# A decoder trunk with split float32 products: the low halves of the output weights by ACT and an adding transfer from POOL

## The chip, the core and the metric

The kernel runs on one core of a Trainium2 chip. The metric is the device time of one execution in microseconds (us). A core has five engines that run beside each other, each through its own queue in order: TensorE (PE, matmuls), VectorE (DVE), ScalarE (ACT), GpSimd (POOL) and SyncE (SP). Data moves between HBM, the large memory, and SBUF, the core's working memory, by transfers on 16 DMA engines; SP, ACT and POOL can issue them.

## What is computed

Two layers of a decoder over 256 positions of width 2048, float32. Layer 0 has sparse and sliding-window attention, layer 1 dilated attention; both end in an output projection, and each layer has an MLP:

```
def reference(x, positions, e_w_in, e_w_o, ..., o_w_in, o_w_o, ln1_g, ln1_b, mlp_w1, mlp_w2, ln2_g, ln2_b):
    ...
    for layer in range(DEPTH):
        ...
            y = _even_mixer(x, cos, sin, e_w_in[i], e_w_o[i], ...)   # ends in  o @ w_o
            y = _odd_mixer(x, cos, sin, o_w_in[i], o_w_o[i])         # ends in  o @ w_o
        x = _layer_norm(DN_ALPHA * x + y, ln1_g[layer], ln1_b[layer])
        x = _layer_norm(DN_ALPHA * x + _mlp(x, mlp_w1[layer], mlp_w2[layer]), ln2_g[layer], ln2_b[layer])
    return x
```

The change is about the two products `o @ w_o`, of a 256 x 2048 by a 2048 x 2048 matrix each.

## The kernel before, in words

Every large product is made of three matmuls in the number form F32R, which keeps fewer bits than float32. Each operand is split into a high half, its value rounded to F32R, and a low half, the rest: a x w is taken as a_hi w_hi + a_hi w_lo + a_lo w_hi. `hi_lo` (L122 to L124) does the split: ACT casts the source into the high half (L123), and DVE subtracts the high half from the source into the low half (L124).

The weights stream in chunks. `w_chunks` (L139) goes through the 2048 rows of a weight matrix, for a block of columns. For a block of 512 columns a chunk is 2 x 128 rows, for one of 256 columns 4 x 128 rows: always a tile of 128 partitions x 1024 numbers, 512 KB. For each chunk SP issues the load into a tile `raw` (L150), `hi_lo` writes `wh` and `wl`, and PE runs through it. `raw` has 5 buffers, `wh` and `wl` have 4 each; a step that writes a buffer waits until the last reader of its earlier content is done. `gemm_tok` (L160) runs the three matmuls for each 128 rows and each of the two halves of the 256 positions (L166 with wh, L167 with wl, L168 with wh): 12 matmuls of 512 columns a chunk, or 24 of 256 columns.

`project` (L665) is the output projection of a layer. It has three blocks of 512 columns of 8 chunks each, then `close` (L588). That first loads and splits the last 256 columns (`halves`, L560, by `hi_lo`), then runs one block of 256 columns (4 chunks), and then the last 256 columns from what `halves` prepared, with the layer norm between. Blocks thus make 28 chunks per layer through `w_chunks`. Between the chunks of the first block the generators in `later` (attention heads still to be finished) get their turn by `tick`, and `before` finishes a head when its rows are due. After each block DVE adds the result to the residual (`add_to`, L534).

The code is recorded once; a scheduler then sets each engine's order of instructions, which stays near the order of the code. A wait is a semaphore between engines.

Of the kernel before, what the change touches and what calls it, by code (L numbers as in the profile page):

```python
# [12 lines left out]
F32 = mybir.dt.float32  # L13
F32R = mybir.dt.float32r
I32 = mybir.dt.int32
AF = mybir.ActivationFunctionType
OP = mybir.AluOpType
# [70 lines left out]
def tile_hybrid_trunk(ctx: ExitStack, tc: tile.TileContext, x, positions, e_w_in, e_w_o, nsa_pe_k, nsa_pe_v,  # L88
# [3 lines left out]
    pe, act, dve, pool = nc.tensor, nc.scalar, nc.vector, nc.gpsimd  # L92
# [3 lines left out]
    wp = ctx.enter_context(tc.tile_pool(name="wp", bufs=W_BUFS))  # L96
# [10 lines left out]
    def tick(n):  # L107
        while n > 0 and later:
            try:
                next(later[0])  # L110
                n -= 1
            except StopIteration:
                later.popleft()

    def finish(gen):
        while gen in later:
            tick(1)
# [4 lines left out]
    def hi_lo(hi, lo, src):  # L122
        act.copy(hi, src)  # L123
        dve.tensor_tensor(lo, src, hi.bitcast(F32), op=OP.subtract)  # L124
# [4 lines left out]
    def hpair():  # L129
        return big.tile([128, 16, 2, T], F32R, name="hc")  # L130
# [5 lines left out]
        ts = slice(t * 128, t * 128 + 128)  # L136
        hi_lo(xc[:, c:c + n, 0, ts], xc[:, c:c + n, 1, ts], tp[:, :n])

    def w_chunks(w, row0, segs, order=range(16), before=None, ticks=None):  # L139
        n = sum(b for _, b in segs)  # L140
        ck = 4 if n <= 256 else 2
        order = list(order)
        for i in range(0, 16, ck):
            if before is not None:
                before(order[i:i + ck])
            r0 = row0 + order[i] * 128
            raw = wp.tile([128, ck, n], F32, name="raw", bufs=RAW_BUFS)
            o = 0
            for c0, b in segs:
                nc.sync.dma_start(raw[:, :, o:o + b], w[r0:r0 + ck * 128, c0:c0 + b]  # L150
                                  .rearrange("(a p) n -> p a n", p=128))
                o += b
            wh = wp.tile([128, ck, n], F32R, name="wh")
            wl = wp.tile([128, ck, n], F32R, name="wl")
            hi_lo(wh, wl, raw)
            for k in range(ck):
                yield order[i + k], i + k == 0, i + k == 15, wh[:, k], wl[:, k]
            tick(ticks or (1 if len(later) < LAG else 2))

    def gemm_tok(xc, w, row0, segs, **kw):  # L160
        n = sum(b for _, b in segs)
        acc = [ps.tile([128, 512], F32, name="acc")[:, :n] for _ in range(2)]
        for kt, first, last, wh, wl in w_chunks(w, row0, segs, **kw):
            for t in range(2):
                a, b = xc[:, kt, 0, t * 128:(t + 1) * 128], xc[:, kt, 1, t * 128:(t + 1) * 128]
                pe.matmul(acc[t], lhsT=a, rhs=wh, start=first, stop=False)  # L166
                pe.matmul(acc[t], lhsT=a, rhs=wl, start=False, stop=False)  # L167
                pe.matmul(acc[t], lhsT=b, rhs=wh, start=False, stop=last)  # L168
        return acc

    def gemm_feat(xc, w, row0, col0, n, **kw):
        acc = [ps.tile([128, 512], F32, name="acc") for _ in range(n // 128)]
        for kt, first, last, wh, wl in w_chunks(w, row0, [(col0, n)], **kw):
            for f in range(n // 128):
                fs = slice(f * 128, (f + 1) * 128)
                if not last:
                    pe.matmul(acc[f], lhsT=wh[:, fs], rhs=xc[:, kt], start=first, stop=False)  # L177
                pe.matmul(acc[f][:, 0:T], lhsT=wl[:, fs], rhs=xc[:, kt, 0], start=False, stop=False)  # L178
                if last:
                    pe.matmul(acc[f], lhsT=wh[:, fs], rhs=xc[:, kt], start=False, stop=True)  # L180
        return acc
# [124 lines left out]
    acc = gemm_tok(xc, e_in, 0, [(2048, 256), (3864, 256)], before=first)  # L306
# [9 lines left out]
    acc = gemm_tok(xc, e_in, 0, [(2304, 280)])  # L316
# [205 lines left out]
    oc = hpair()  # L522
# [11 lines left out]
    def add_to(acc, t, c0, n, fac, slot=None):  # L534
        z = xr[:, t, c0:c0 + n]
        dve.scalar_tensor_tensor(z, z, fac, acc, op0=OP.mult, op1=OP.add)  # L536
        if slot is not None:
            dve.bn_stats(st[t][:, slot], z)

    def load_gb(g_in, b_in, i):  # L540
        gb = big.tile([128, 2, D], F32, name="gb", tag="sgb")
        nc.sync.dma_start(gb[:, 0], g_in[i:i + 1].to_broadcast([128, D]))
        nc.sync.dma_start(gb[:, 1], b_in[i:i + 1].to_broadcast([128, D]))
        return gb
# [120 lines left out]
    def project(w, order, need, gin, bin_, i, nxt):  # L665
        def before(kts):
            if kts[0] in need:
                finish(need[kts[0]])

        def block(c0, n, slot):  # L670
            acc = gemm_tok(oc, w, 0, [(c0, n)], order=order, before=before, ticks=3)
            for t in range(2):
                add_to(acc[t], t, c0, n, ALPHA, slot)

        block(0, 512, 0)
        gb = load_gb(gin, bin_, i)
        block(512, 512, 1)
        block(1024, 512, 2)
        return close(oc, w, 0, ALPHA, gb, block, nxt)
# [53 lines left out]
    oc = hpair()  # L733
# [64 lines left out]
    for hb in range(4):  # L798
# [14 lines left out]
        for g in range(3):  # L813
            lo = 256 if hb + g == 0 else 0
            acc = gemm_tok(xc, o_in, 0, [(g * 6144 + 4096 + hb * 512 + lo, 512 - lo)])
# [34 lines left out]
```

## Time and profile before

| | |
|---|---|
| median of 2 runs | 2775.53 us (2775.29 to 2775.78) |
| span of the profiled execution | 2773.8 us |
| PE busy | 2748.2 us (99%) |
| DVE busy | 1686.6 us (61%) |
| ACT busy | 1239.0 us (45%) |
| POOL busy | 44.4 us (2%) |
| DMA moved | 509 MB, 184 GB/s in the mean |

The span is that of one execution with the profiler on; the median is of executions without it. An engine's busy time is the time in which it has an instruction under way; a matmul's own duration (0.39 us for 512 columns) overlaps its neighbours', so the pace is read from the starts, which are 0.227 us apart. "Idle before, releaser" says what ended an engine's wait. The DMA share is the mean busy share of the 16 DMA engines; it can come out a little above 1. The granted clock of PE is 1.00 at 2.4 GHz and 0.50 at 1.2 GHz.

### The profile page before, as it was taken

What the parts mean: (1) busy time and instruction counts of PE and PEld (TensorE: products, weight loads), DVE (VectorE), ACT (ScalarE), POOL (GpSimd) and SP (SyncE); (2) the same over time, 40 slices, a digit from 0 to 9 for tenths busy, and PEclk for the clock granted to TensorE, in tenths of its full rate; (3) what the DMA queues carried; (4) which work ended last, traced back from release to release, by engine and by line L of the source; (5) the groups of instructions that cost most, each with busy time, mean ns of one, the idle gap of its engine ahead of it and who ended that gap; (6) DMA issues with size and microseconds to landing.
All of it is one profiled execution on the core that took longest, in us unless ns stands there. A gap on an engine that the chain in (4) does not pass through costs nothing.

```text
span 2773.8 us, 37579 instructions
## 1 busy us (share of the span) xinstructions
PE 2748.2 (99%) x14840; PEld 2362.4 (85%) x14840; DVE 1686.6 (61%) x2281; ACT 1239.0 (45%) x1648; POOL 44.4 (2%) x40
## 2 busy tenths in 40 slices
PE   9999999999999999999999999999999999999997
PEld 7888888888888889888888888888898888888887
DVE  6667665455555556774774675576565455565556
ACT  5345444344443444444444445445444344443442
POOL 0000010000000001000000000000010000000001
PEclk9999999999999999999999999999999999999999
DMA  8743655665666665555555456455566665665653
GB/s 275 200 136 118 224 175 189 193 188 191 190 189 193 187 195 166 178 179 164 175 182 176 152 183 197 155 179 185 195 197 188 192 189 189 191 189 191 189 190 130
DMA packets 283985, 509.18 MB, mean 184 GB/s; under 512 B 15840, under 2 KB 61184, under 8 KB 282528
## 3 DMA queue, kind: packets, MB, share of 16 engines
q1 hardware_dynamic: 283248, 506.02, 58.9%
q8 instruction: 116, 1.90, 0.3%
q10 hardware_dynamic: 432, 0.59, 0.1%
q14 instruction: 61, 0.50, 0.0%
q0 software_dynamic: 128, 0.16, 0.0%
HBM read 504.62 MB, written 2.10 MB: 183 GB/s over the span
## 4 chain that ended last, share of the span: by engine, by line
PE 85%; issue 9%; DVE 1%; POOL 1%; ACT 0%; POOLq 0%
PE acc L177 28%; PE acc L178 15%; PE acc L168 12%; PE acc L166 12%; PE acc L167 12%; PE acc L180 2%; PE sc L743 1%; PE acc L586 1%; PE acc L584 1%; PE acc L585 1%; PE po L784 1%; PE tp L772 1%; DVE xr L621 0%; POOL xr L622 0%; PE po L780 0%
## 5 line engine op out<-in xcount | busy, mean ns | idle before, releaser
L124 DVE TENSOR_TENSOR wl<-raw,wh 128x1024 fp32r<-128x1024 f32 (+1 forms) x932 | 1133.2, 1220 | 941.0 <-ACT wh L123 938.5
L123 ACT CAST wh<-raw 128x1024 fp32r<-128x1024 f32 (+1 forms) x932 | 976.7, 1049 | 1327.1 <-PE acc L177 684.3
L177 PE MATMUL acc<-xc,wh 128*128 128x512 f32 x3690 | 1315.9, 400 | 1.1 <-DVE qk L185 1.1
L178 PE MATMUL acc<-xc,wl 128*128 128x256 f32 x3936 | 1094.1, 281 | 0.0
L177 PEld LDWEIGHTS acc<-xc,wh 128*128 128x128 f32 x3690 | 693.2, 188 | 166.6 <-DVE qk L185 1.8
L178 PEld LDWEIGHTS acc<-xc,wl 128*128 128x128 f32 x3936 | 743.4, 189 | 5.9
L166 PE MATMUL acc<-wh,hc 128*128 128x512 f32 (+1 forms) x1280 | 485.7, 379 | 0.0
L167 PE MATMUL acc<-wl,hc 128*128 128x512 f32 (+1 forms) x1280 | 484.7, 379 | 0.0
L168 PE MATMUL acc<-wh,hc 128*128 128x512 f32 (+1 forms) x1280 | 484.6, 379 | 0.0
L167 PEld LDWEIGHTS acc<-wl,hc 128*128 128x128 f32 x1280 | 240.8, 188 | 45.1
L168 PEld LDWEIGHTS acc<-wh,hc 128*128 128x128 f32 x1280 | 240.8, 188 | 44.9
L166 PEld LDWEIGHTS acc<-wh,hc 128*128 128x128 f32 x1280 | 240.9, 188 | 44.3
L166 PE MATMUL acc<-wh,xc 128*128 128x512 f32 (+2 forms) x448 | 170.4, 381 | 0.0
L167 PE MATMUL acc<-wl,xc 128*128 128x512 f32 (+2 forms) x448 | 168.6, 377 | 0.0
L168 PE MATMUL acc<-wh,xc 128*128 128x512 f32 (+2 forms) x448 | 168.0, 376 | 0.0
L166 PEld LDWEIGHTS acc<-wh,xc 128*128 128x128 f32 x448 | 84.6, 189 | 15.6 <-ACT xc L123 1.4
L168 PEld LDWEIGHTS acc<-wh,xc 128*128 128x128 f32 x448 | 84.6, 189 | 15.3 <-DVE xc L124 0.2
L167 PEld LDWEIGHTS acc<-wl,xc 128*128 128x128 f32 x448 | 84.7, 189 | 15.2 <-DVE wl L124 0.8
L180 PE MATMUL acc<-xc,wh 128*128 128x512 f32 x246 | 88.7, 395 | 0.0
L254 DVE TENSOR_TENSOR ropeB<-qk,sinT 64x512 f32<-64x512 f32 x120 | 82.3, 686 | 2.3
L536 DVE SCALAR_TENSOR_TENSOR xr<-xr,acc 128x512 f32<-128x512 f32 (+1 forms) x88 | 52.7, 633 | 23.6 <-PE acc L586 15.0
L184 ACT COPY qk<-acc 128x256 f32<-128x256 f32 x122 | 42.8, 373 | 30.8 <-PE acc L180 30.8
(187 smaller groups left out, 1491.4 us busy)
## 6 DMA issues: line engine op xcount, KB each, us to landing
raw<-in_mlp_w_dram SPq DMA_DIRECT2D x512, 512.0 KB, 3.8
raw<-in_o_w_in_dram SPq DMA_DIRECT2D x288, 512.0 KB, 3.7
raw<-in_e_w_in_dram SPq DMA_DIRECT2D x52, 512.0 KB, 4.4
raw<-in_e_w_o_dram SPq DMA_DIRECT2D x32, 512.0 KB, 3.6
raw<-in_o_w_o_dram SPq DMA_DIRECT2D x32, 512.0 KB, 4.5
raw<-in_e_w_in_dram SPq DMA_DIRECT2D x16, 256.0 KB, 6.2
gb<-in_ln_g_dram SPq DMA_DIRECT2D x4, 1024.0 KB, 4.7
gb<-in_ln_b_dram SPq DMA_DIRECT2D x4, 1024.0 KB, 7.5
```

The costliest lines, as they stand in the source:

```text
L123: act.copy(hi, src)
L124: dve.tensor_tensor(lo, src, hi.bitcast(F32), op=OP.subtract)
L166: pe.matmul(acc[t], lhsT=a, rhs=wh, start=first, stop=False)
L167: pe.matmul(acc[t], lhsT=a, rhs=wl, start=False, stop=False)
L168: pe.matmul(acc[t], lhsT=b, rhs=wh, start=False, stop=last)
L177: pe.matmul(acc[f], lhsT=wh[:, fs], rhs=xc[:, kt], start=first, stop=False)
L178: pe.matmul(acc[f][:, 0:T], lhsT=wl[:, fs], rhs=xc[:, kt, 0], start=False, stop=False)
L180: pe.matmul(acc[f], lhsT=wh[:, fs], rhs=xc[:, kt], start=False, stop=True)
L184: act.copy(dst, acc[:, T:2 * T])
L254: dve.tensor_tensor(B[o:o + 64], dst[i:i + 64], sinT[i:i + 64, perm][:, None].to_broadcast([64, h, T]), op=OP.mult)
L536: dve.scalar_tensor_tensor(z, z, fac, acc, op0=OP.mult, op1=OP.add)
L584: pe.matmul(acc, lhsT=a, rhs=wh, start=kt == 0, stop=False)
```

## The change

In the blocks of the two output projections (`block` in `project`, with the new argument `summed=True`) the low half of the weights is made in another way. ACT casts `raw` into `wh` as before; then ACT writes -wh into `wl`, and POOL issues a transfer that adds `raw` to `wl` where it lies. The 4 chunks per layer of `halves`, and all other products, keep `hi_lo`.

```
-    def w_chunks(w, row0, segs, order=range(16), before=None, ticks=None):
+    def w_chunks(w, row0, segs, order=range(16), before=None, ticks=None, summed=False):
...
             wh = wp.tile([128, ck, n], F32R, name="wh")
-            wl = wp.tile([128, ck, n], F32R, name="wl")
-            hi_lo(wh, wl, raw)
+            if summed:
+                wl = wp.tile([128, ck, n], F32R, name="wl")
+                act.copy(wh, raw)
+                act.mul(wl, wh.bitcast(F32), -1.0)
+                pool.dma_start(wl, raw, accum_op=OP.add)
+            else:
+                wl = wp.tile([128, ck, n], F32R, name="wl")
+                hi_lo(wh, wl, raw)
...
         def block(c0, n, slot):
-            acc = gemm_tok(oc, w, 0, [(c0, n)], order=order, before=before, ticks=3)
+            acc = gemm_tok(oc, w, 0, [(c0, n)], order=order, before=before, ticks=3, summed=True)
```

Where that puts the instructions, at two places. ACT in the second block of layer 0's projection, before (the number behind a name tells the buffers' contents apart):

```order
L123 CAST wh_2784<-raw_2782 128x1024
L123 CAST wh_2802<-raw_2800 128x1024
L123 CAST wh_2820<-raw_2818 128x1024
L123 CAST wh_2838<-raw_2836 128x1024
L123 CAST wh_2862<-raw_2860 128x1024
```

and the same engine and place in the changed kernel:

```order
L156 CAST wh_2796<-raw_2794 128x1024
L156 CAST wh_2815<-raw_2813 128x1024
L157 ACTIVATE wl_2797<-wh_2796 128x1024
L157 ACTIVATE wl_2816<-wh_2815 128x1024
L156 CAST wh_2834<-raw_2832 128x1024
L157 ACTIVATE wl_2835<-wh_2834 128x1024
L156 CAST wh_2853<-raw_2851 128x1024
L157 ACTIVATE wl_2854<-wh_2853 128x1024
```

Each cast has a multiplication behind it now; in one place of this block two casts come before their two multiplications, elsewhere they alternate.

POOL from its last load of small weights to the first layer norm, before:

```order
L336 DMA pen<-in_nsa_pe_k_dram 32x128
L338 DMA w2s<-in_nsa_ck_w_dram 128x128
L551 ISA
L551 TENSOR_TENSOR rs_3235<-mv_3234,neghalf 128x1
L622 TENSOR_TENSOR xr<-xr,gb 128x512 x3
```

and in the changed kernel:

```order
L342 DMA pen<-in_nsa_pe_k_dram 32x128
L344 DMA w2s<-in_nsa_ck_w_dram 128x128
L158 DMA wl<-raw 128x1024 x28
L557 ISA
L557 TENSOR_TENSOR rs_3263<-mv_3262,neghalf 128x1
L628 TENSOR_TENSOR xr<-xr,gb 128x512 x3
```

28 transfers stand ahead of the layer norm's work, and 28 more at the same place of layer 1. PE's matmuls keep their order within a chunk (wh, wl, wh), and SP's loads keep theirs; a load into `raw` now waits for the transfer that read the buffer's earlier content.

## Rows read from the trace of the kernel before

**Rows 1.** The page, its span and part 1: busy us, share, instructions.

```profile
span 2773.8 us, 37579 instructions
PE 2748.2 (99%) x14840; PEld 2362.4 (85%) x14840; DVE 1686.6 (61%) x2281; ACT 1239.0 (45%) x1648; POOL 44.4 (2%) x40
```

**Rows 2.** Windows of the two projections: length, busy us, clock, DMA share, GB/s.

```profile
core 0: us, PE busy (x) PEld busy (x) DVE busy (x) ACT busy (x) POOL busy (x), PEclk, DMA share, GB/s
251.60:343.20 91.60, 91.43 (x474) 77.77 (x473) 64.92 (x118) 47.84 (x84) 0.00 (x0) 1.00 0.62 201
...
1942.63:2030.50 87.87, 87.87 (x466) 75.58 (x465) 47.92 (x49) 40.22 (x54) 0.00 (x0) 1.00 0.64 210
```

**Rows 3.** Timeline of ACT in layer 0's third block: start, us, instruction, idle before.

```profile
299.19 1.05 ACT L123 CAST wh<-raw 128x1024 fp32r<-128x1024 f32 x1 [1.67 <-PE acc L168]
301.91 1.05 ACT L123 CAST wh<-raw 128x1024 fp32r<-128x1024 f32 x1 [1.67 <-PE acc L168]
304.63 1.05 ACT L123 CAST wh<-raw 128x1024 fp32r<-128x1024 f32 x1 [1.67 <-PE acc L168]
```

**Rows 4.** Timeline of DVE, the same place.

```profile
300.28 1.23 DVE L124 TENSOR_TENSOR wl<-raw,wh 128x1024 fp32r<-128x1024 f32 x1 [1.49 <-ACT wh L123]
303.00 1.22 DVE L124 TENSOR_TENSOR wl<-raw,wh 128x1024 fp32r<-128x1024 f32 x1 [1.49 <-ACT wh L123]
305.72 1.23 DVE L124 TENSOR_TENSOR wl<-raw,wh 128x1024 fp32r<-128x1024 f32 x1 [1.50 <-ACT wh L123]
```

**Rows 5.** Waits of SP's queue, 250 to 345 us: total us, times, longest.

```profile
SPq L150 <- DVE wl L124: 53.0, 21, 5.8
SPq L565 <- DVE wl L124: 16.0, 8, 3.1
```

**Rows 6.** Loads of the output weights, layer 0, then layer 1: issue to landing.

```profile
DMA to landing us min/median/max: 3.3/3.6/6.3
...
DMA to landing us min/median/max: 3.5/4.5/7.1
```

**Rows 7.** Timeline of ACT in the first layer norm: three activations together.

```profile
351.81 2.23 ACT L620 ACTIVATE xr<-xr,nmr,rs 128x512 f32<-128x512 f32 x3 [7.42 <-DVE nmr L599]
```

**Rows 8.** Timeline of POOL: its issues of 128-row loads.

```profile
2.00 0.57 POOL L338 DMA_DIRECT2D w2s<-in_nsa_cv_w_dram  x1
...
106.57 0.56 POOL L338 DMA_DIRECT2D w2s<-in_nsa_ck_w_dram  x1 [25.40 <-PE pv L381]
```

**Rows 9.** Windows at the program's start, where loads queue: columns as rows 2.

```profile
5.00:10.00 5.00, 3.65 (x12) 1.85 (x11) 2.12 (x4) 2.61 (x6) 0.00 (x0) 1.00 1.06 351
10.00:15.00 5.00, 4.99 (x18) 4.06 (x19) 3.44 (x6) 2.53 (x4) 0.00 (x0) 1.00 1.06 345
```

**Rows 10.** DMA issues from POOL: count, KB each, us to landing.

```profile
w2s<-in_nsa_cv_w_dram POOLq DMA_DIRECT2D x1, 64.0 KB, 4.5
w2s<-in_nsa_ck_w_dram POOLq DMA_DIRECT2D x1, 64.0 KB, 2.1
```

**Rows 11.** Windows around the end of PE's work: columns as rows 2.

```profile
2755.00:2760.00 5.00, 4.77 (x40) 4.57 (x39) 4.52 (x8) 1.52 (x2) 3.18 (x3) 1.00 0.13 48
2760.00:2765.00 5.00, 0.00 (x0) 0.00 (x0) 4.42 (x9) 0.27 (x1) 1.84 (x2) 0.89 0.44 163
2765.00:2774.00 9.00, 0.00 (x0) 0.00 (x0) 5.05 (x5) 1.25 (x2) 3.11 (x2) 0.50 0.31 117
```

**Rows 12.** Timeline of PE near the program's start.

```profile
11.03 0.63 PE L167 MATMUL acc<-wl,xc 128*128 128x512 f32 x1
11.46 0.63 PE L168 MATMUL acc<-wh,xc 128*128 128x512 f32 x1
...
12.73 0.41 PE L168 MATMUL acc<-wh,xc 128*128 128x512 f32 x1
12.98 0.39 PE L166 MATMUL acc<-wh,xc 128*128 128x512 f32 x1
13.22 0.40 PE L167 MATMUL acc<-wl,xc 128*128 128x512 f32 x1
```

## The prediction

> **What bounds the kernel now.** I read the page first. TensorE (PE) is busy for 2748.2 of 2773.8 us, VectorE (DVE) for 61% and ScalarE (ACT) for 45% [rows 1]. A mean can hide a stage with another limit, so the two stretches that the change touches are read alone. PE works on the output products of layer 0 from 251.6 to 343.2 us and of layer 1 from 1942.63 to 2030.5 us. In them it is busy for 91.43 of 91.60 us and for 87.87 of 87.87 us, at a granted clock of 1.00; the 16 DMA engines are busy for 0.62 and 0.64 of the time [rows 2]. So PE is the limit there too, and 0.17 us is all that a faster supplier of weights could give back.
>
> Next, who waits for whom. In the even part ACT starts a cast every 2.72 us, the time of a chunk's twelve matmuls, and each was released by PE, which had finished with the chunk four before [rows 3]. DVE subtracts right behind it, for 1.23 us, and idles 1.49 us between [rows 4]. The supply is thus held back by its four buffers: a low half is ready some 2.3 us (1.05 + 1.23) after PE frees its buffer, and is needed three chunks (8.2 us) after that. It is early by nearly 6 us. What SP's loads wait for is DVE's subtraction, which frees the raw tile [rows 5]; a load lands 3.3 to 6.3 us after its issue in layer 0, 3.5 to 7.1 us in layer 1 [rows 6].
>
> **The change part by part.** Each layer has 28 such chunks, 56 in all (three blocks of 8 and one of 4).
>
> DVE loses 56 subtractions of 1.23 us, 69 us of work. It idles between them, and PE waited for none of them: worth 0.
>
> ACT gains 56 multiplications. The trace has no such row over 1024 columns; below stands the cast of the same shape (1.05 us, [rows 3]), above twice an activation over 512 columns (2.23 / 3 = 0.74 us, so 1.49 us, [rows 7]). ACT would be busy for 2.1 to 2.5 us of each 2.72. I take 1.05; either hides behind PE, and the multiplication waits for nothing that the cast did not wait for.
>
> POOL gains 56 issues. Its issue of a 128-row load takes 0.56 us [rows 8] and it has no other work in these stretches: 0 on PE's path.
>
> The transfers themselves are the term that counts. Each adds 512 KB to the work of the same 16 DMA engines. What is left of them: 91.60 x (1 - 0.62) + 87.87 x (1 - 0.64) = 34.8 + 31.6 = 66.4 us. At the program's start the share goes up to 1.06, with 351 GB/s [rows 9], so the books may hold 6% more: 77 us. Divided by 56 that is 1.19 to 1.38 us for each transfer. The nearest row for its price is a 512 KB load at that rate: 524,288 bytes / 351 GB/s = 1.49 us, at a share of 1.06, so 1.58 us of all engines. That is the bound from below: 56 x 1.58 = 88.5, over by 11 to 22 us. But an adding transfer fetches two tiles, the raw one and the negated one, for one that it writes. If fetching is what engines spend their time on, the price is 3.17 us and the sum 177 us, over by 100 to 111 us. No row shows an adding transfer. I take the price of two fetches, as nothing in the profile lets the second be free, and 105 us.
>
> The Trainium skill (Collectives: The Full Stack, section "The bandwidth ceiling: the fold count and why AG ≠ RS ≠ AR") says the same of an add in the DMA engines: it is slow not by the arithmetic but since each chunk is read from two sources. By that page's 31 GB/s per engine, halved, 16 engines would take an estimated 2.1 us for 512 KB and the excess would be some 50 us, a time near 2827; no run here has shown it. Its DMA: Bandwidth & Descriptors (section "Issuing engines are not separate DMA queues") says that transfers from POOL share the 16 engines with SP's; here no row can show that yet.
>
> Waits. The multiplication waits on ACT for its buffer; behind it stand the next casts, and in the first eight chunks the attention's exponentials and copies. POOL's transfer waits for the multiplication; nothing of POOL's is urgent behind it. SP's load of a raw tile now waits until the transfer that read it five chunks earlier has landed, with all later loads behind it in SP's queue, those of the MLP's first weights too. PE waits for the low half at a chunk's second matmul. Round the four buffers a chunk costs (2.72 + 2.1 + L) / 4, with L from POOL's issue to landing. Nothing is late as long as L stays under 6.1 us. L is at least 0.56 + 3.3, on empty engines. With two fetches, a load and an add take 1.58 + 3.17 = 4.75 us a chunk, and at that pace the buffers allow L up to 14 us: the engines, not the buffers, set the pace. Being early saves once per layer what is in hand at its start: from 0 to 8 us, I take 4, so 8 in all.
>
> Sum: 2773.8 us of the profiled execution, 1.7 us around it (the median is 2775.5), + 105 - 8 = 2872 us.
>
> **The rivals.**
>
> (a) The transfers hide. If the second fetch and the write run beside the first, the price is 1.58 us, and 11 to 22 us are left, less the 8: a time of 2779 to 2790. For it: a share of 1.06 shows that the books are not exact, and tiles in SBUF may come faster than weights from HBM. Against it: even this price is over what is free. It decides the sign: the loss passes 2% (55.5 us) where a transfer costs more than (66.4 + 55.5 + 8) / 56 = 2.3 us of all engines.
>
> (b) The transfers go one by one. If POOL's next transfer starts only when the one before has landed, a layer lasts at least 28 x (0.56 + landing). With landings of 3.3, about 4.05 (the mean of the medians) and 7.1 us that is 108, 129 and 214 us for stretches of 91.6 and 87.9: + 37, + 79 and + 249, so 2812, 2854 and 3025. For it: 64 KB from POOL took 4.5 and 2.1 us to land [rows 10], far more than their bytes need. Against it: in the program's first microseconds loads overlapped [rows 9].
>
> (c) PE's clock falls. After PE's last matmul the granted clock went to 0.89 in the next 5 us and 0.50 after that [rows 11]; at the program's start, after idling, a 128x512 matmul followed the one before by 0.43 us, and by 0.24 us from 12.7 us on [rows 12]. Those are its levels of 1.2 and 2.4 GHz. A chunk at the lower one takes 5.4 us where the transfers ask for 4.75: the twenty plain chunks of a layer would give another 14 us, in all some 2900. Against it: the expected wait is some 2 us in each chunk, not 5 on end. The Trainium skill (TensorE: Matmul & The Clock Gate, section "What's actually happening") says the same, that an idle PE is throttled.
>
> (d) The time falls, as DVE is freed. PE has 0.17 us to give in the stretches: at best 2775.
>
> That the change does nothing of what it says is excluded: the 28 transfers per layer stand in POOL's order, and DVE's subtractions are gone.
>
> **How the numbers follow.** Two fetches, engines full: 0.42, 2840 to 2910. (a): 0.27, all within 2%. (b): 0.22, of which 0.03 within 2%. (c): 0.06. (d) and the rest: 0.03, of which 0.01 faster. Slower by over 2%: 0.42 + 0.19 + 0.06 = 0.67; within 2%: 0.27 + 0.03 + 0.02 = 0.32; faster: 0.01. (2% is about what a measurement of this kernel can tell from no change.) The forecast is that of the first case, 2872. The range is 2785 to 3010: it leaves out the lower half of (a), the top of (b), and prices above two fetches, some 0.2 together.
>
> **What would show it.** Right: in both stretches the DMA share stands at 1.0 or above, the even chunks come every 4.5 to 5 us, PE waits at a wl matmul, and ACT's casts wait for loads or for PE; DVE is some 69 us less busy; the rest of the kernel keeps its times. (a) is right if casts still come every 2.72 us. (b) is right if POOL's transfers do not overlap and the DMA share stays under 0.9 while PE waits. (c) shows as a granted clock under 1.00. I am wrong in the size if an add costs other than two loads, and wrong in the place if the loss lies outside the stretches.

## The result and the profile after

The changed kernel takes 2845.45 us (median of 2 runs, 2842.51 to 2848.38), the kernel before 2775.53 us: a ratio of 1.0252, 95% interval 1.0222 to 1.0281. It is slower by 70 us, on the side that was forecast and some 27 us under the forecast itself. One run further below, of the kernel with every second chunk, took 7055.59 us in place of some 2805 us and is left out of its time.

The page of the kernel after, span and part 1 (beside [rows 1]):

```profile
span 2840.7 us, 37760 instructions
PE 2766.9 (97%) x14840; PEld 2368.1 (83%) x14840; DVE 1620.3 (57%) x2225; ACT 1293.8 (46%) x1704; POOL 93.6 (3%) x96
```

DVE is 66.3 us less busy, ACT 54.8 us more, POOL 49.2 us more. PE has the same 14840 matmuls and is busy 18.7 us longer. Where the time went is seen in the two projection stretches, from the first matmul with `hc` to the last of the fourth block (windows of the kernel after, columns as [rows 2]; the last two are the first block and the three others of layer 0):

```profile
251.45:378.57 127.12, 105.54 (x509) 85.75 (x508) 36.14 (x93) 71.87 (x109) 22.41 (x26) 0.95 1.00 252
1974.58:2098.00 123.42, 100.18 (x500) 80.92 (x499) 16.15 (x22) 64.20 (x79) 22.59 (x26) 0.97 1.02 262
251.45:297.90 46.45, 42.15 (x205) 34.89 (x204) 20.30 (x74) 32.28 (x70) 7.59 (x9) 0.96 0.96 245
297.90:378.57 80.67, 63.39 (x306) 50.87 (x305) 15.85 (x19) 39.60 (x40) 14.82 (x17) 0.94 1.01 257
```

Against [rows 2] the stretches are 35.5 us longer each. Of that, 4.3 us are only moved: 36 matmuls of the closing 256 columns (L590 to L592, 0.12 us each), which stood behind the fourth block before, now stand ahead of it. The true loss is read where the closing's second half is added to the residual (timeline of DVE, layer 0, first before, then after):

```profile
356.29 0.40 DVE L536 SCALAR_TENSOR_TENSOR xr<-xr,acc 128x256 f32<-128x256 f32 x1
```

```profile
388.52 0.40 DVE L542 SCALAR_TENSOR_TENSOR xr<-xr,acc 128x256 f32<-128x256 f32 x1
```

From the start of the stretch that is 104.7 and 137.1 us: 32.4 us lost in layer 0, and by the same rows of layer 1 (100.9 and 135.1) 34.2. Together they are 66.6 of the 66.9 us by which the span grew; the rest of the kernel keeps its times. The DMA engines, 0.62 and 0.64 busy before, are at 1.00 and 1.02. PE now stands idle for 21.6 us of the first stretch, and it is busy for 14.1 us more: 4.3 for the moved matmuls, the other 9.8 at a granted clock of 0.95.

Who waits for whom now: the waits of SP's queue, then PE's, from 250 to 380 us (us in total, times, longest; beside [rows 5]).

```profile
SPq L150 <- DMA wl<-raw: 83.5, 21, 9.5
SPq L571 <- DMA wl<-raw: 26.8, 6, 7.6
```

```profile
PE acc L173 <- DMA wl<-raw: 21.6, 14, 4.3
```

SP's loads, which waited for DVE's subtraction, wait for the adding transfer, and PE waits at L173, the matmul with `wl`. The chain of waits of the kernel after, a part of 300 to 350 us (start, us, what):

```profile
303.81 10.71 DMA raw<-in_e_w_o_dram
...
317.04 6.74 DMA wl<-raw
323.77 0.02 SPq L150
...
323.84 10.41 DMA raw<-in_e_w_o_dram
...
343.29 6.92 DMA wl<-raw
```

It goes from a load to an add and, through the raw buffer that the add frees, to the next load: DMA but for some 2.4 us between a load and its add, in which ACT casts and multiplies, and with 10 us for a load that landed in 3.6 us before [rows 6].

The transfers themselves, on the page of the kernel after (queue: packets, MB, share of 16 engines' span) and in the view of line 158:

```profile
q0 software_dynamic: 8192, 29.53, 5.4%
```

```profile
L158 POOL DMA_DIRECT2D wl<-raw x56: 862/872/916, 238.2 to 2085.3; - x56
...
DMA to landing us min/median/max: 4.6/7.8/11.8
```

A share of 5.4% of 2840.7 us over 56 transfers is 2.74 us of all 16 engines for one of them (2.71 to 2.76 with the rounding of the share). A load of 512 KB from HBM takes 1.69 us by the same arithmetic on the page of the kernel before (58.9% of 2773.8 us for 506.02 MB).

### The profile page after: what moved, and what is told of

It is laid out like the page before. It is cut to its first block, busy times and chain, and to the rows that moved or that the text cites. A ratio compares the mean times of both kernels' runs of the same rounds, so it can differ in the third digit from the quotient of the medians.

```text
span 2840.7 us, 37760 instructions
## 1 busy us (share of the span) xinstructions
PE 2766.9 (97%) x14840; PEld 2368.1 (83%) x14840; DVE 1620.3 (57%) x2225; ACT 1293.8 (46%) x1704; POOL 93.6 (3%) x96
## 3 DMA queue, kind: packets, MB, share of 16 engines
q1 hardware_dynamic: 283248, 506.02, 58.0%
## 4 chain that ended last, share of the span: by engine, by line
PE 87%; DMA 5%; issue 2%; DVE 1%; POOL 1%; ACT 0%; POOLq 0%; SPq 0%; DVEq 0%; ACTq 0%
PE acc L183 29%; PE acc L184 16%; PE acc L173 11%; PE acc L174 11%; PE acc L172 11%; DMA wl<-raw 2%; PE acc L186 2%; DMA raw<-in_o_w_o_dram 1%; PE sc L749 1%; DMA raw<-in_e_w_o_dram 1%; PE acc L592 1%; PE tp L778 0%; PE acc L590 0%; PE acc L591 0%; PE po L790 0%
## 5 line engine op out<-in xcount | busy, mean ns | idle before, releaser
L124 DVE TENSOR_TENSOR wl<-raw,wh 128x1024 fp32r<-128x1024 f32 (+1 forms) x876 | 1065.2, 1219 | 955.1 <-ACT wh L123 951.9
L123 ACT CAST wh<-raw 128x1024 fp32r<-128x1024 f32 (+1 forms) x876 | 918.1, 1048 | 1272.6 <-PE acc L183 676.5
L173 PE MATMUL acc<-wl,hc 128*128 128x512 f32 (+1 forms) x1280 | 491.9, 384 | 44.8 <-DMA wl<-raw 44.8
L173 PEld LDWEIGHTS acc<-wl,hc 128*128 128x128 f32 x1280 | 243.3, 190 | 102.0 <-DMA wl<-raw 57.4
L173 PE MATMUL acc<-wl,xc 128*128 128x512 f32 (+2 forms) x448 | 168.8, 377 | 0.0
L173 PEld LDWEIGHTS acc<-wl,xc 128*128 128x128 f32 x448 | 84.9, 189 | 15.2 <-DVE wl L124 0.7
L156 ACT CAST wh<-raw 128x1024 fp32r<-128x1024 f32 x56 | 58.2, 1045 | 77.9 <-PE acc L174 27.3
L158 POOL DMA_DIRECT2D wl<-raw x56 | 48.9, 874 | 1178.8 <-ACT wl L157 996.0
```

The lines of the kernel that those rows point to most:

```text
L156: act.copy(wh, raw)
L158: pool.dma_start(wl, raw, accum_op=OP.add)
```

## The experiments

The times of before that each group shared were 2775.47, 2775.89 and 2775.50 us. The losses below are against those. E stands for the theory that engine time decides; the first four expectations call it A, and the rival by which the raw buffers decide B.

**The extra step on ACT alone.** ACT still writes -wh, and DVE does the addition.

```
-                pool.dma_start(wl, raw, accum_op=OP.add)
+                dve.tensor_tensor(wl, raw, wl.bitcast(F32), op=OP.add)
```

> ACT casts and multiplies as in the change, but DVE adds raw to wl in SBUF; no POOL transfer. Theories A and B (the transfer alone costs): 2774 to 2782 us, the time of the kernel before, as ACT's 1.06 us more per chunk lie behind PE. Theory D (the step added on ACT, or two casts ahead of two multiplications, is what makes PE wait): more than 2800 us.

Measured: 2776.07 us, ratio 1.0002 (0.9993 to 1.0012). The 56 multiplications and their place in ACT's order cost nothing by themselves, with DVE as busy as before. What costs is the transfer.

**A copy in place of the add.** The same transfer without the addition, so that the low halves hold the whole weights.

```
-                pool.dma_start(wl, raw, accum_op=OP.add)
+                pool.dma_start(wl, raw)
```

> The POOL transfer copies raw into wl and adds nothing (so the low halves hold the whole weights: that part of the computation is changed), with the same bytes written, the same waits and the same buffers. Theory A (the 16 DMA engines are full, and the second fetch of an adding transfer is what fills them): a copy costs about a load, 1.6 to 1.7 us of all engines, 56 of them 90 to 95 us against 66 to 77 us free, so 2780 to 2800 us, and the DMA share in the projections stays near 1. Theory B (the raw tiles are held too long: load, cast, multiplication and transfer in a row round five buffers): the row of waits is as long as before but for what the engines are less full, 2815 to 2845 us. Theory C (adding is not dearer than copying): 2845 us as in the changed kernel.

Measured: 2804.52 us, ratio 1.0104 (1.0089 to 1.0119), a loss of 29 us, 5 us above the range of A and 10 us under that of B. Its page says of the queue:

```profile
q0 software_dynamic: 8192, 29.53, 3.0%
```

3.0% of 2802.2 us over 56 is 1.50 us a copy, against 2.74 for an add of the same bytes. So 41 us of the 70 are due to the addition, and 29 to there being a transfer at all.

**Every second chunk.** Only the odd chunks use the transfer, the others DVE's subtraction.

```
-            if summed:
+            if summed and i // ck % 2:
```

> Only every second chunk of the blocks takes the new way, 28 transfers in all; the others are split by DVE as before. Theory A (the engines overflow): 28 x 2.5 to 2.74 us = 70 to 77 us against 66 to 77 us free, so nearly nothing is over: 2775 to 2790 us. If each transfer had its own price on PE's path, half of the loss would stay: 2810 us. Theory B (buffers): a raw tile is held long in every second chunk only, five buffers then go round in about 16 us, 3.2 us a chunk: 2790 to 2805 us.

Measured: 2804.61 us, ratio 1.0098 (1.0078 to 1.0118), a loss of 29 us. By the stretch as a whole 28 x 2.8 = 78 us fit into the 77 us that were free, and nearly nothing should have been lost: A missed by 15 to 30 us, while the range of B (2790 to 2805) holds the result. The windows of this kernel show where the time went:

```profile
280.00:290.00 10.00, 6.26 (x28) 4.86 (x27) 3.85 (x12) 3.72 (x11) 0.00 (x0) 0.83 0.72 207
290.00:347.00 57.00, 49.40 (x205) 39.72 (x206) 19.70 (x22) 29.23 (x31) 6.08 (x7) 0.93 0.87 243
```

In the first row PE has a single wait, of 3.74 us, in the attention's part. It ends at 284.78 us, as a low half lands whose cast and transfer stand so in the timelines of ACT and POOL:

```profile
275.27 1.04 ACT L156 CAST wh<-raw 128x1024 fp32r<-128x1024 f32 x1 [1.67 <-PE acc L174]
```

```profile
277.70 0.87 POOL L158 DMA_DIRECT2D wl<-raw  x1 [5.83 <-DVE nm L286]
```

The cast itself waited until PE freed its buffer, and the transfer then took some 7 us from its issue: PE came to the low half before that. In the second row, 0.87 of the engines' time is used. Two ideas came out of it: that free time counts only where it lies, block by block, and that there is a further loss in ACT's order and in so short a lead. The next runs take them apart.

**More raw buffers.** The raw tiles of the 512-column blocks come from eight buffers in the space of the layer's input halves.

```
-            raw = wp.tile([128, ck, n], F32, name="raw", bufs=RAW_BUFS)
+            if summed and n == 512:
+                j = spare["j"] = (spare["j"] + 1) % 8
+                raw = spare["t"][:, j].rearrange("p (a n) -> p a n", a=ck)
+            else:
+                raw = wp.tile([128, ck, n], F32, name="raw", bufs=RAW_BUFS)
...
```

> The changed kernel, but the raw tiles of the three blocks of 512 columns come from a ring of eight in memory that is free at this time (the space of xc), in place of five. Theory A (engines full): the bytes are the same, so 2832 to 2848 us, with the DMA share still at 1 in the projections. Theory B (the row load, cast, multiplication, transfer of some 20 us round the raw buffers): 20 / 8 = 2.5 us a chunk, so only the four wl buffers bind, (2.72 + 2.1 + 7.8) / 4 = 3.2 us: 2790 to 2805 us.

Measured: 2854.12 us, ratio 1.0283 (1.0268 to 1.0298). This does not decide alone: the space comes free only at about 250 us, so the first loads were late (PE was busy for 1.79 us of 10 from 260 us on). In the next kernel only the second and third block get the eight buffers:

```
         block(0, 512, 0)
+        spare["t"] = big.tile([128, 8, 1024], F32, name="spare", tag="xc")
+        spare["j"] = -1
...
```

> The kernel after, with the raw tiles of the second and third block of each output product taken from eight buffers of their own (in the space of the layer's input halves, which is free by then), so that a raw tile that its transfer still reads holds up no load; the first block keeps the common buffers. Theory E (the engines are full at a share of 1.0 in blocks two to four, more buffers give them nothing to fill): 2835 to 2850. Rival B (the five raw buffers, held about 20 us from load to the end of the add, pace the loop): 2790 to 2825.

Measured: 2852.97 us, ratio 1.0280 (1.0265 to 1.0295), some 7 us slower than after. The view of its transfers:

```profile
DMA to landing us min/median/max: 4.5/8.5/12.6
```

The transfers land later, and the whole is no faster. But the loss moved. By DVE's additions to the residual layer 0 has its first block 14.0 us later than in the kernel after (311.96 and 297.95 us) and is 7.0 us faster from there to the last one (83.5 and 90.6 us). The loads of the later blocks, and those of the closing halves, now run into the attention's part; ACT stands at casts whose loads have not landed, and PE waits there for the attention's steps, which in the kernel after it does not (timeline of PE):

```profile
275.70 1.22 PE L433 MATMUL po<-pT,vv 128*128 128x256 f32 x2 [4.62 <-ACT pT L428]
291.04 0.79 PE L402 MATMUL sc<-qk 128*128 128x128 f32 x2 [5.25 <-DVE nm L292]
```

To the end of layer 0's fourth block the engines are busy for 0.96 of 132.45 us here and for 0.99 of 127.45 us in the kernel after, 127 and 126 us: more buffers do not lessen their time. That they could not help, were the attention left alone, is argued from the share of 1.00 in the kernel after and not shown by this run.

**The price by itself.** The kernel before, with three adds from POOL, three copies from SP and three copies from POOL at its end, each group after the one before.

```
...
+                for k in (3, 4, 5):
+                    pool.dma_start(pr[:, k].bitcast(F32R), pr[:, 0], accum_op=OP.add)
+                for k in (6, 7, 1):
+                    nc.sync.dma_start(pr[:, k], pr[:, 5])
+                for k in (2, 3, 4):
+                    pool.dma_start(pr[:, k].bitcast(F32R), pr[:, 1])
```

> The kernel before, with nine transfers of 512 KB inside the on-chip memory put at its very end, where the engines of the DMA are idle: three that add (issued by POOL, as in the change), then three plain copies issued by SP, then three plain copies issued by POOL; each group waits for the one before it. They move scratch data and are extra work, so the total time says nothing. Theory E (an add occupies all sixteen engines 2.74 us because it fetches two sources, also where no load runs beside it): the group of adds takes 3 x 2.6 to 2.9 us = 8 to 9 us from its first issue plus a fixed delay of about 2, with the share of the engines near 1; a group of copies takes 3 x 1.5 = 4.5 us plus that delay, the same for both issuers. Rival Q (the adds are long because they go one by one, each waiting for the one before or for its own read of the target; the engines are not full): the group of adds takes 3 x 4.5 to 7 = 13 to 21 us with a share well under 0.8, the copies 3 x 3 us. Rival S (an add is slow only beside loads from the main memory): adds cost 1.5 us each here, as the copies.

Measured, in the view of DMA by queue: first the 14 us of the adds (2731 to 2745; q1 carries the last loads beside them), then the 7.5 us of the copies from SP (2744 to 2751.5), then the 6 us of those from POOL (2750 to 2756).

```profile
q0 software_dynamic: 432, 1.57, 57.0%
q1 hardware_dynamic: 1491, 1.48, 31.3%
```

```profile
q1 hardware_dynamic: 432, 1.57, 53.0%
```

```profile
q0 software_dynamic: 429, 1.56, 74.7%
```

The same 1.57 MB take 57.0% of 14 us = 7.98 us as adds, 3.98 us as copies from SP and 4.48 us as copies from POOL: 2.66, 1.33 and 1.49 us each. And the windows of 1 us, one in the adds after the loads, one in the copies from SP, one in those from POOL (columns as [rows 2], the last two the DMA share and GB/s):

```profile
2740.00:2741.00 1.00, 1.00 (x11) 1.00 (x10) 1.00 (x2) 0.00 (x0) 0.00 (x0) 1.00 1.04 205
2747.00:2748.00 1.00, 1.00 (x11) 1.00 (x10) 0.00 (x0) 0.00 (x0) 0.00 (x0) 1.00 1.01 397
2754.00:2755.00 1.00, 1.00 (x10) 1.00 (x10) 0.37 (x1) 0.00 (x0) 0.00 (x0) 1.00 1.12 397
```

The engines are full in all three; an add fills them at 205 GB/s, a copy at 397. In the first row no load is left beside the adds, and 512 KB at 205 GB/s and a share of 1.04 are 2.66 us again. The three adds were issued within 2.75 us and took 8.6 us each (median) to land, so they run beside each other. E holds; that they go one by one, and that they are dear only beside loads, falls. Whether the second read or the addition itself makes an add twice as dear, no run separates.

**ACT's order at the end.** The high halves of the closing 256 columns are cast by DVE, so that no late load stands between a cast and its multiplication on ACT.

```
-            hi_lo(wh, wl, raw)
+            if spare:
+                dve.tensor_copy(wh, raw)
+                dve.tensor_tensor(wl, raw, wh.bitcast(F32), op=OP.subtract)
+            else:
+                hi_lo(wh, wl, raw)
```

> The kernel after, with one edit: the high halves of the closing 256 columns of each projection are cast by DVE (66 us less busy than before) in place of ACT, so that no cast of these late chunks stands in ACT's queue between a block chunk's cast and its multiplication. Transfers, loads and sums are those of after. Theory E (the DMA engines are full, and PE's loss is their surplus work): no change, 2842 to 2850. Theory T (a good part of the loss in the third and fourth block comes from ACT standing at a cast whose load is late while a multiplication behind it is ready, some 6 us at about 330 us and again in the second layer): 2830 to 2838.

Measured: 2843.57 us (2843.03 to 2844.72), ratio 1.0245 (1.0230 to 1.0260), within the spread of after (2842.51 to 2848.38) and in E's range. In this kernel that order costs a few us at most.

**Two of four blocks, and one of four.** The transfers only in the second and third block, or only in the first.

```
-            acc = gemm_tok(oc, w, 0, [(c0, n)], order=order, before=before, ticks=3, summed=True)
+            acc = gemm_tok(oc, w, 0, [(c0, n)], order=order, before=before, ticks=3, summed=slot in (1, 2))
```

> The kernel after, with the adding transfers only in the second and third block of each output product (32 of 56); the first block (beside the attention) and the fourth (256 columns, beside the closing halves) take DVE's subtraction, as before. Theory E, by engine time: a chunk asks 1.7 us for its load and 2.74 for its add, 4.44 us at a share of 1.0 against PE's 2.72, so 16 chunks lose 27 us a layer less what the loads that run ahead save (some 7 us): about 2815, 2803 to 2825. By the blocks of after (the second took 23.5 us in place of 21.6, the third 35.3 in place of 21.9) it would be 15 us a layer: 2806. Rival P (the loss is one of places, the short lead in the attention part and ACT's order at the end, not of engine time): under 2790.

Measured: 2821.60 us, ratio 1.0171 (1.0154 to 1.0188), a loss of 46 us, in E's range. With `summed=slot == 0`:

> The kernel after, with the adding transfers only in the first block of each output product (16 of 56), the block that runs beside the end of the attention and whose engines were 0.42 busy before; the other three take DVE's subtraction. Theory E, by engine time: 8 adds of 2.74 us are 22 us a layer and 21 us were free there, so they fit or nearly: 2775 to 2781. Rival W (a lead too short: casts and multiplications stand late in ACT's order there, and 7 us from issue to landing in place of DVE's 1.23 are waited for): one or two waits of about 4 us a layer and PE slower after each, 2784 to 2796; the upper end is what the first block lost in after, 10 us a layer.

Measured: 2781.91 us, ratio 1.0021 (1.0012 to 1.0031), a loss of 6 us, 1 us above E's range and 2 us under the rival's. Windows of layer 0's first block in these two kernels, that without transfers first:

```profile
251.45:288.00 36.55, 34.94 (x177) 28.57 (x176) 24.40 (x76) 24.50 (x61) 2.66 (x3) 1.00 0.57 155
```

```profile
251.45:290.00 38.55, 38.54 (x200) 32.28 (x199) 23.98 (x77) 29.57 (x69) 5.22 (x6) 1.00 0.90 226
```

Sixteen adds beside the attention raise the engines to 0.90 there and cost 6 us in all, 0.4 us each; thirty-two in the plain blocks cost 46 us, 1.4 us each. In the first block most of the adds find free time, in the others most do not. The 6 us are not spread evenly: layer 0 is 1.7 us longer than before, by the closing addition as above, and the rest lies in layer 1, where PE has one wait for a low half (timeline):

```profile
1975.80 0.80 PE L173 MATMUL acc<-wl,hc 128*128 128x512 f32 x1 [4.26 <-DMA wl<-raw]
```

That is the single wait of some 4 us that the rival W expects; the engines were full around it too (a share of 1.04 from 1970 to 1980 us), so the run does not tell a short lead from full engines there.

**Half the bytes, the same count.** Each transfer adds half of the chunk, DVE the other half.

```
-                pool.dma_start(wl, raw, accum_op=OP.add)
+                h = ck // 2
+                pool.dma_start(wl[:, h:], raw[:, h:], accum_op=OP.add)
+                dve.tensor_tensor(wl[:, :h], raw[:, :h], wl[:, :h].bitcast(F32), op=OP.add)
```

> The kernel after, with each of the 56 transfers half as large: it adds the second half of the chunk's rows (256 KB), and DVE adds the first half. Count, order and waits of the transfers stay, their bytes are halved. Theory E (engine time decides, by bytes): as with half of the transfers at full size, a chunk asks 1.7 + 1.37 = 3.1 us of the engines in place of 4.44: 2795 to 2812. Rival Q (the fixed path of each transfer, POOL's issue and the wait for its landing, decides): 2835 to 2848, since all 56 are still there.

Measured: 2803.31 us, ratio 1.0099 (1.0082 to 1.0116), a loss of 28 us: bytes decide, not the number of transfers. The group of line 159 in the view by line shows POOL's issues, which did not get cheaper:

```profile
L159 POOL DMA_DIRECT2D wl<-raw x56 | 48.9, 874 | 1152.8 <-ACT wl L157 976.3 <-PE po L514 131.4 <-ACT hc L123 12.7
```

**Fewer loads, the same adds.** Two chunks, or all chunks of a block, share one raw tile and its load.

```
-            raw = wp.tile([128, ck, n], F32, name="raw", bufs=RAW_BUFS)
+            if not summed or i // ck % 2 == 0:
+                raw = wp.tile([128, ck, n], F32, name="raw", bufs=RAW_BUFS)
...
```

The load below it moves into the condition too; in the second kernel the condition ends in `i == 0`.

> The kernel after, without every second load of weights of the chunks that use the adding transfer (two neighbouring chunks share one raw tile, so 28 of 56 loads of 512 KB are left out and the products use the wrong rows). All 56 adding transfers stay. Theory E: a chunk asks (1.7 / 2) + 2.74 = 3.6 us of the engines in place of 4.44, against PE's 2.72: the loss falls from 70 to between 30 and 48, 2805 to 2823. Rival Q (the path of a transfer decides, not the load beside it): 2838 to 2848.

Measured: 2829.36 us, ratio 1.0197 (1.0181 to 1.0212), a loss of 54 us, 6 us above E's range and 9 under the rival's.

> The kernel after, with one load of weights per block in place of one per chunk (8 of the 56 loads are left, all chunks of a block use the same raw tile, so the products use the wrong rows). All 56 adding transfers stay, and a cast waits for no load. Theory E: a chunk asks little more than the 2.74 us of its add, which is PE's own 2.72 per chunk; only the fourth block is over, where the closing halves are loaded (four adds and eight loads, 24 us against 11.7): 2780 to 2800. Rival Q (a transfer's 0.87 us of issue and 7.8 us to landing, four buffers): 2830 or more, since nothing of that is changed.

Measured: 2800.20 us, ratio 1.0089 (1.0074 to 1.0104), a loss of 25 us, at the top of E's range. With all 56 adds in place the loss falls from 70 to 54 and 25 us as loads are taken off the engines: it is the sum of both that PE waits for (a load that is gone also needs no waiting for; the two are not apart here). The products of both kernels use the rows of another chunk. Why the first of the two lies above its range is seen on ACT (timeline, start, us, what, idle before):

```profile
314.36 1.05 ACT L157 CAST wh<-raw 128x1024 fp32r<-128x1024 f32 x1 [0.57 <-PE acc L175]
320.82 1.04 ACT L123 CAST wh<-raw 128x1024 fp32r<-128x1024 f32 x1 [5.41 <-DMA raw<-in_e_w_o_dram]
321.78 1.05 ACT L158 ACTIVATE wl<-wh 128x1024 fp32r<-128x1024 f32 x1
```

The multiplication was ready at 315.4 and came at 321.8, behind a cast of the closing halves (L123) whose load had not landed; right behind it the engines ran dry (a window from 322 to 324 us had a share of 0.02). ACT's order costs something here that it did not cost in the kernel after, where the engines had no free time to lose. How much was not measured by a run.

**All of them in one table.** Free engine time, from windows of the kernel before, each against a full share of 1.06 [rows 9]. The boundary leaves the other blocks the 55 us that their 20 chunks take; the first block's own result stands at 291.67 us in layer 0, as some matmuls of the second run ahead of it:

```profile
251.60:288.00 36.40, 36.23 (x185) 30.10 (x184) 28.95 (x81) 22.81 (x60) 0.00 (x0) 1.00 0.42 134
288.00:343.20 55.20, 55.20 (x291) 47.67 (x290) 35.96 (x37) 25.03 (x24) 0.00 (x0) 1.00 0.74 244
1942.63:1975.40 32.77, 32.77 (x178) 27.97 (x177) 11.74 (x13) 15.00 (x30) 0.00 (x0) 1.00 0.56 193
1975.40:2030.50 55.10, 55.10 (x290) 47.62 (x289) 36.17 (x37) 25.23 (x24) 0.00 (x0) 1.00 0.69 220
```

That is 36.40 x 0.64 + 32.77 x 0.50 = 40 us in the two first blocks and 55.20 x 0.32 + 55.10 x 0.37 = 38 us in the others. "Asked" is the transfers by the price on the kernel's own page, less 1.69 us for each load left out. The table was made after the runs; the price and the loss are measured, the rest is worked out.

| kernel | price, us | asked, first blocks | asked, others | over, by blocks | over, both pooled | loss |
|---|---|---|---|---|---|---|
| after | 2.74 | 44 | 110 | 4 + 72 = 76 | 76 | 70 |
| copy | 1.50 | 24 | 60 | 22 | 6 | 29 |
| every second chunk | 2.80 | 22 | 56 | 18 | 0 | 29 |
| half the bytes | 1.50 | 24 | 60 | 22 | 6 | 28 |
| second and third block | 2.73 | 0 | 87 | 49 | 9 | 46 |
| first block | 2.78 | 44 | 0 | 4 | 0 | 6 |
| half of the loads | 2.77 | 31 | 77 | 39 | 30 | 54 |
| one load a block | 2.80 | 21 | 54 | 16 | 0 | 25 |
| more raw buffers | 2.75 | 44 | 110 | 76 | 76 | 77 |

By blocks the loss comes out within 15 us for every kernel; pooled over the whole stretch it fails by 22 to 37 us wherever less is asked of those blocks, and by 6 for the first block alone. It holds for the sum and not for its parts: by the starts of DVE's additions the first blocks of the kernel after lose 6.4 us in layer 0 and 6.0 in layer 1, 12 together, and the others 54, where the table has 4 and 72. By the end of layer 0's first block POOL had issued 11 adds, at least three of them for the second block, and so part of the others' surplus is paid in the first.

## Why the prediction was right, and where it was off

**The bound, and the freed DVE.** Right: DVE is freed of 66 us (69 forecast), and in the stretches of before PE had 0.17 us of waiting to give back. No run frees DVE without a transfer; with DVE kept busy and the transfers taken out, the rest of the change moves nothing (1.0002).

**ACT.** Right: a multiplication takes 1.06 us (1.05 taken) and is hidden.

**POOL.** Off in the size, right in the path: an issue takes 0.87 us in place of 0.56. With all 56 issues kept and half the bytes the loss fell to 28 us, so they are not what PE waits for.

**The price of an add.** This is the term that was mis-sized: 3.17 us were taken, 2.74 measured (2.66 alone). The factor was right: an add fills the engines about twice as long as a copy of the same bytes (1.33 and 1.49 alone, 1.50 in the stretch; 1.58 was the bound from below). That the second fetch is its reason fits, and is not shown by itself. The rest is the base: a copy inside SBUF is cheaper than the row at 351 GB/s from HBM that was doubled. The Trainium skill (Collectives: The Full Stack, section "The bandwidth ceiling: the fold count and why AG ≠ RS ≠ AR") explains a factor of two, between collectives, by two reads; the run has that factor, 205 against 397 GB/s. The estimate from the rate on that page of the Trainium skill, 2.1 us, was too low by 0.6, and the time near 2827 also left out the 8 us for being early. The Trainium skill (DMA: Bandwidth & Descriptors, section "Issuing engines are not separate DMA queues") has transfers of all issuers run on the same 16 engines; the trace agrees: POOL's adds and SP's loads fill them to 1.00 together.

**The free time.** With 2.74 in place of 3.17 the sum of the prediction gives 153 less 66 to 77, less 8: 2844 to 2854, against 2845 measured. That it fits so well is in part luck. The 8 us for being early are in it, which no run measured. And the step summed the free time of a whole stretch, and free time can't be carried from the attention's part to the plain blocks. By the table it makes no difference in the kernel after, because the first blocks' own adds ask for 44 us where 40 are free; with half of the adds it makes 18 us.

**The pace and the waits.** The forecast was 4.75 us a chunk. DVE's additions to the residual give the ends of the blocks, the first three of layer 0 in the kernel before and then all four in the kernel after (timelines):

```profile
291.67 1.28 DVE L536 SCALAR_TENSOR_TENSOR xr<-xr,acc 128x512 f32<-128x512 f32 x2
309.58 1.28 DVE L536 SCALAR_TENSOR_TENSOR xr<-xr,acc 128x512 f32<-128x512 f32 x2
331.52 1.28 DVE L536 SCALAR_TENSOR_TENSOR xr<-xr,acc 128x512 f32<-128x512 f32 x2
```

```profile
297.95 1.37 DVE L542 SCALAR_TENSOR_TENSOR xr<-xr,acc 128x512 f32<-128x512 f32 x2 [3.98 <-PE acc L174]
321.49 1.37 DVE L542 SCALAR_TENSOR_TENSOR xr<-xr,acc 128x512 f32<-128x512 f32 x2 [20.97 <-PE acc L174]
356.73 1.37 DVE L542 SCALAR_TENSOR_TENSOR xr<-xr,acc 128x512 f32<-128x512 f32 x2 [3.06 <-PE acc L174]
378.91 0.75 DVE L542 SCALAR_TENSOR_TENSOR xr<-xr,acc 128x256 f32<-128x256 f32 x2
```

Between the rows of after the second block takes 23.5 us, the third 35.2 (4.4 a chunk), the fourth 22.2, with 4.3 us of closing matmuls in it (4.5 a chunk); between those of before the second takes 17.9 and the third 21.9. An add and a load are 2.74 + 1.69 = 4.43 us, the pace of the last two. The second block, part of whose matmuls and adds come ahead of the first row, lost 5.6 us only. Casts no longer come every 2.72 us as in [rows 3] but in bursts, released by loads or by PE (timeline of ACT, the kernel after):

```profile
306.62 1.05 ACT L156 CAST wh<-raw 128x1024 fp32r<-128x1024 f32 x1 [2.06 <-PE acc L174]
307.71 1.06 ACT L157 ACTIVATE wl<-wh 128x1024 fp32r<-128x1024 f32 x1
314.60 1.05 ACT L156 CAST wh<-raw 128x1024 fp32r<-128x1024 f32 x1 [5.83 <-DMA raw<-in_e_w_o_dram]
```

That the engines and not the buffers set the pace fits: the share is 1.00, landings of up to 11.8 us stayed under the 14 that the buffers allow, and more raw buffers made the whole no faster, though that run also disturbed the attention.

**The rivals.** (a) falls: the share is 1.00, and 2.74 us lies above the 2.3 from which the loss passes 2%. (b) falls: adds overlap, and one by one the landing of 7.8 us would have given 28 x 8.7 = 243 us a layer, not 127. (d) falls. (c) happened in part: the clock was 0.95 and 0.97 in the stretches, and PE's busy time grew by 14.1 and 12.3 us, 9.8 and 8.0 of them not moved work. The loss (70 us) is not larger than the engines' surplus (76) all the same, so the lower clock added nothing to it that can be seen. That a slower PE would only wait less where the engines are full is argued; no run held the clock. Where they are not, a lower clock may be a part of the 6 to 15 us by which five kernels of the table lose more than their surplus, with ACT's order and the short lead; no run took these three apart, and that stays open.

## What to carry to other kernels

A transfer that replaces an engine's work is paid in time of the DMA engines, which the weight stream already uses: work out its price (an add costs two copies) and compare it with what is free in that part of the kernel, not in the mean and not over a longer stretch than the buffers can reach across. Work taken off an engine that nobody waits for has nothing to give back: here 66 us of DVE against 0.17 us of PE's waiting. A calibration in an idle corner of the same kernel gives the price to a few per cent, before anything is rebuilt.

## What the hardware showed that was not expected

- An add of 512 KB inside SBUF takes 2.66 us of all 16 engines (205 GB/s written), a copy 1.33 us from SP's queue and 1.49 us from POOL's.
- POOL issues an adding transfer in 0.87 us and a plain one in 0.53 us, and an add of 256 KB costs as much to issue as one of 512 KB (0.87 us).
- After a wait of 3.74 us PE's matmuls start 0.43 us apart in place of 0.23, at a granted clock of 0.50 (285 to 286 us), the lower of its two levels. The timeline of PE in the kernel with every second chunk:

```profile
279.75 0.39 PE L172 MATMUL acc<-wh,hc 128*128 128x512 f32 x1
279.97 0.39 PE L173 MATMUL acc<-wl,hc 128*128 128x512 f32 x1
...
284.78 0.80 PE L173 MATMUL acc<-wl,hc 128*128 128x512 f32 x1 [3.74 <-DMA wl<-raw]
285.38 0.63 PE L174 MATMUL acc<-wh,hc 128*128 128x512 f32 x1
285.80 0.63 PE L173 MATMUL acc<-wl,hc 128*128 128x512 f32 x1
```
